# A two-layer hybrid decoder trunk on eight cores: hand-ordered engine queues with stage barriers replaced by one graph of operations under a static list scheduler

## The chip, the cores and the metric

The program runs on the 8 cores of one Trainium2 chip, one batch element per core; the cores do not talk to each other. The time is the device time of the slowest core, in microseconds (us). Fast runs of one kernel mostly agree within about 0.4%. Some runs fall into a slower state, in which the cores of one die, or of both, show a lower clock of the tensor engine. Only fast runs are compared here unless the text says otherwise.

Engines are named as in the profile: PE does matmuls, PEld loads their weights, DVE is VectorE, ACT is ScalarE, POOL is GpSimd, SP issues DMAs. PEclk is the clock granted to PE, as a share of full speed. The trace's clock records begin with a kernel's first dense work (at 183.6 us in the kernel before); ahead of that a view prints 1.00, which is not a measurement.

## The reference, cut to what matters

Each core has x of 4096 positions by 1024 features in fp32. Matmuls are in bf16, sums in fp32. The kernels work in 8 tiles of 512 positions and in four stages, called here M0 (mixer of layer 0), F0 (its MLP), M1 (mixer of layer 1) and F1 (second MLP and final norm).

```python
def reference(x, c, ada_w, ada_b, ...):
    for layer in range(DEPTH):                                   # DEPTH = 2
        sh1, sc1, g1, sh2, sc2, g2 = ada_modulation(c, ada_w[layer], ada_b[layer])   # silu(c) @ (1024 x 6144)
        h = rmsnorm(x, norm_mix_g[layer]) * (1.0 + sc1) + sh1
        if layer % 2 == 0:
            p = jnp.einsum('bsd,de->bse', h, w_in0[j])           # 3584 columns
            a_b, a_c, a_h, b_q, b_f, b_i, b_g = jnp.split(p, IN0_SPLITS, axis=-1)
            y_a = short_conv_mixer(a_b, a_c, a_h, conv_w[j], conv_b[j])
            y_b = hgrn2_mixer(b_q, b_f, b_i, b_g, lower_bounds[layer], hg_gain[j])
            y = jnp.einsum('bse,ed->bsd', jnp.concatenate([y_a, y_b], axis=-1), w_out0[j])
        else:
            z = jax.nn.gelu(jnp.einsum('bsd,de->bse', h, w_in1[j]) + b_in1[j])
            y = spatial_gating_mixer(z, gm_ln_g[j], gm_ln_b[j], gm_ws[j], gm_bs[j])
            y = jnp.einsum('bse,ed->bsd', y, w_out1[j])
        x = x + g1 * y
        h = rmsnorm(x, norm_ffn_g[layer]) * (1.0 + sc2) + sh2
        hid = jnp.square(jax.nn.relu(jnp.einsum('bsd,df->bsf', h, w_ff1[layer])))    # 4096 columns
        x = x + g2 * jnp.einsum('bsf,fd->bsd', hid, w_ff2[layer])
    return rmsnorm(x, final_g)
```

HGRN2 is a gated linear recurrence in chunks of 64 positions. Within a chunk it needs the running sum `cum` of the log forget gates, and the products of queries and keys with `exp(cum)`, `exp(-cum)` and `exp(last - cum)`.

## The kernel before

Operations are put on five queues, one per engine, **in the order in which the Python program makes them**. Each waits for the semaphores of what it reads and overwrites. Overlap is what the author wrote by hand with generators, and every stage ends with a barrier that only weight loads may cross.

```python
class Prog:
    def op(self, qn, fn, reads=(), writes=(), dsem=None):
        q = self.q[qn]
        for b in reads:
            if b.w is not None:
                self._wait(qn, b.w)
        for b in writes:
            for t in b.r.values():
                self._wait(qn, t)
            if b.w is not None:
                self._wait(qn, b.w)
        # ... (cut: append to the queue, count the semaphore up, set b.w and b.r)
```

The RMSNorm (L366 squares, a matmul with a constant matrix that sums over features, L376 scaling on VectorE, L379 shift on ScalarE):

```python
        def norm_and_modulate(xT, xTb, sqt, sqb, tmp, tmpb, hT, hb, invB, b_inv, ...):
            for c in range(8):
                P.op("act", lambda e, ...: e.activation(out=sqt[:, c % 2, :], in_=src_ap, func=AF.Square),
                     reads=[src_b], writes=[sqb[c % 2]])
                P.op("pe", lambda e, c=c: mm(e, ps[:, nbank, :], onesD[:], sqt[:, c % 2, :], c == 0, c == 7), ...)
            rsqrt_eps(invB[:], b_inv, ps[:, nbank, :], b_norm_bank)
            for c in range(8):
                P.op("dve", lambda e, c=c: e.scalar_tensor_tensor(
                    out=tmp[:, c % ntmp, :], in0=xT[:, c, :], scalar=scol(l, which, c), in1=invB[:],
                    op0=ALU.mult, op1=ALU.mult), ...)
                P.op("act", lambda e, c=c: e.activation(out=hT[:, c, :], in_=tmp[:, c % ntmp, :], func=AF.Identity, ...)
```

The MLP computes the next tile's norm between two halves of its own matmuls, so that part of it is hidden (L865 relu, L867 square of it):

```python
                    ff2(0, xT, xTb)
                    for _ in ff1(1):
                        pass
                    if ti + 1 < ntiles:
                        norm_and_modulate(xT2[:, 1 - cur], xTb2[1 - cur], ...)     # next tile
                    ff2(1, xT, xTb)
```

The adaLN modulation is a prologue of 24 pieces of 2 MB of fp32 weights that ends before anything else starts (a barrier follows it). The HGRN2 gates make every decay by its own subtraction, clipping and exponential; per head and tile that is one scan and eleven full-size VectorE passes, and seven ScalarE passes:

```python
                        P.op("dve", ... S_ft[:, 0] = cum3 - cum3[:, :, 63:64] ...)      # to the chunk's end
                        P.op("act", ... S_ft[:, 0] = Exp(-S_ft[:, 0]) ...)
                        P.op("dve", ... S_kd = S_ft[:, 2] * S_ft[:, 0] ...)
                        P.op("dve", ... S_ft[:, 1] = cum4 - S_cref2 ...)                # to the middle of the chunk
                        P.op("act", ... S_ft[:, 1] = Exp(S_ft[:, 1]) ...)
                        # ... (cut: two more of this kind, then q times two of the factors)
```

(The argument lists are shortened to formulas in this last block.) x comes in position-major and is transposed on PE in fp32 (L494), and transposed back at the end (L897).

The softmax here doesn't subtract the row's maximum and nothing guards it: scores larger than these inputs give would overflow.

## Time and profile before

| | |
|---|---|
| time | 4312.05 us, median of 3 runs (4309.94 to 4314.02) |
| profiled span, slowest core | 4319.8 us |
| PE busy, mean granted clock | 73%, 0.85 |

From the page of the kernel before: busy time and share of the span per engine; the span in 40 slices, with the busy tenths of PE and the tenths of the granted clock; and last the chain of work that ended last, by engine.

```profile
PE 3138.2 (73%) x15143; PEld 1426.2 (33%) x15143; DVE 1577.8 (37%) x3025; ACT 1302.1 (30%) x2085; POOL 60.4 (1%) x75
PE   1166465475564649999999975757664999999997
PEclk9887677686676769999999997878877999999998
PE 62%; ACT 11%; DVE 10%; DMA 9%; issue 7%; DVEq 0%; ACTq 0%; POOL 0%; SPq 0%; POOLq 0%
```

The tensor engine has the most work, but it is idle a quarter of the time, and 15 of the 40 slices show a clock digit of 7 or 6. The chain says that 62% of the span is PE's own work; the rest of the chain is other engines' work, DMA and issue.

Busy time of each engine in eight stretches of the kernel before: prologue, M0, change, F0, change, M1, change, F1. The columns are the stretch and its length, busy us and instructions of PE, PEld, DVE, ACT and POOL, then granted clock, DMA share and GB/s.

```profile
0.00:165.00 165.00, 23.48 (x738) 21.84 (x738) 2.36 (x13) 2.99 (x4) 21.33 (x28) 1.00 1.12 157
165.00:1542.00 1377.00, 788.33 (x3968) 370.14 (x3968) 653.19 (x1273) 507.36 (x800) 15.40 (x18) 0.73 0.16 36
1542.00:1570.00 28.00, 0.00 (x0) 0.00 (x0) 0.00 (x0) 0.00 (x0) 3.19 (x5) 0.56 0.88 198
1570.00:2571.00 1001.00, 935.97 (x4160) 410.44 (x4160) 249.73 (x448) 243.71 (x400) 7.49 (x9) 0.95 0.17 44
2571.00:2600.00 29.00, 1.88 (x6) 0.92 (x6) 4.36 (x11) 1.58 (x3) 0.00 (x0) 0.53 0.79 235
2600.00:3244.00 644.00, 422.76 (x1856) 182.22 (x1855) 317.51 (x640) 288.96 (x415) 4.97 (x6) 0.79 0.17 51
3244.00:3290.00 46.00, 4.42 (x8) 0.83 (x8) 1.66 (x3) 7.35 (x12) 4.26 (x6) 0.51 1.01 223
3290.00:4320.00 1030.00, 961.34 (x4408) 439.79 (x4408) 348.98 (x638) 250.11 (x452) 3.71 (x5) 0.95 0.13 37
```

The mixers are the loose stages: in M0 PE is busy 788 of 1377 us at clock 0.73. The MLPs are nearly dense. The changes cost 28, 29 and 46 us. Per tile the stages take about 170 (M0), 122.9 (F0), 78.6 (M1) and 125.8 us (F1).

The longest of PE's waits in the kernel before (engine, tile, line, and what ended the wait: us in total, times, longest).

```profile
PE ps L220 <- DVE sb_arena L1104: 160.0, 47, 7.8
PE ps L220 <- ACT sb_arena L366: 156.1, 121, 38.0
PE ps L220 <- DMA sb_arena<-ada_w: 136.6, 24, 7.3
```

L1104 is the spatial gating of M1, L366 are the squares of the norm, and `ada_w` is the prologue. They are serial chains; the change supposes that PE could do other work in the meantime, if the queue order let it.

### The profile page before, as it was taken

The numbers are of one execution on the slowest core, as the hardware profiler recorded it, in microseconds if no ns is written. First come the engines' busy times: TensorE is split into PE (matmuls) and PEld (weight loads), VectorE is DVE, ScalarE is ACT, GpSimd is POOL, SyncE is SP. The second block draws the span as 40 slices with busy tenths as digits, with TensorE's granted clock in tenths as the row PEclk, the third lists the DMA queues.
The fourth block names the chain that finished last, engine by engine and source line by source line (L and its number), as shares of the span: only waits on it lengthen the run. The fifth ranks groups of instructions, "written<-read, shape, count | busy, mean of one in ns | idle before, by whom it ended". The sixth has DMA issues, their size and how long they took to land.

```text
span 4319.8 us, 45196 instructions; the slowest of 8 cores (4287.9 to 4319.8 us)
## 1 busy us (share of the span) xinstructions
PE 3138.2 (73%) x15143; PEld 1426.2 (33%) x15143; DVE 1577.8 (37%) x3025; ACT 1302.1 (30%) x2085; POOL 60.4 (1%) x75
## 2 busy tenths in 40 slices
PE   1166465475564649999999975757664999999997
PEld 1132232232222214444444432323222444444443
DVE  0154444444444522222222214454551333333333
ACT  0143333433433422222222204444531222222221
POOL 1100000000000000000000000000000000000000
PEclk9887677686676769999999997878877999999998
DMA  9920010010001470011111230211139001111100
GB/s 157 160 50 20 20 40 20 20 39 20 20 20 39 69 145 21 20 40 39 40 40 40 48 74 29 75 39 60 58 61 178 15 25 40 40 40 40 40 16 25
DMA packets 126001, 213.73 MB, mean 49 GB/s; under 512 B 2640, under 2 KB 59728, under 8 KB 125776
## 3 DMA queue, kind: packets, MB, share of 16 engines
q0 software_dynamic: 65648, 74.45, 11.9%
q1 hardware_dynamic: 60128, 136.39, 9.0%
q8 instruction: 128, 2.10, 0.2%
q14 instruction: 97, 0.79, 0.1%
HBM read 218.17 MB, written 67.11 MB: 66 GB/s over the span
## 4 chain that ended last, share of the span: by engine, by line
PE 62%; ACT 11%; DVE 10%; DMA 9%; issue 7%; DVEq 0%; ACTq 0%; POOL 0%; SPq 0%; POOLq 0%
PE ps L220 61%; DMA sb_arena<-ada_w 3%; DMA xs<-sb_arena 2%; ACT sb_arena L366 2%; DVE sb_arena L1104 2%; DVE sb_arena L733 2%; DVE sb_arena L376 2%; ACT sb_arena L379 1%; DMA sb_arena<-x 1%; DMA sb_arena<-xs 1%; DMA sb_arena<-w_in 1%; ACT sb_arena L214 1%; ACT sb_arena L216 1%; ACT sb_arena L737 1%; PE ps L897 1%
## 5 line engine op out<-in xcount | busy, mean ns | idle before, releaser
L220 PE MATMUL ps<-sb_arena 128*128 128x512 bf16 (+4 forms) x14209 | 2899.1, 365 | 809.2 <-DVE sb_arena L1104 160.0
L220 PEld LDWEIGHTS ps<-sb_arena 128*128 128x128 bf16 x14209 | 1307.8, 102 | 2387.4 <-issue 1072.5
L865 ACT ACTIVATE sb_arena<-ps 128x512 bf16<-128x512 f32 x512 | 303.1, 596 | 1262.6 <-PE ps L220 1231.5
L867 DVE TENSOR_TENSOR sb_arena<-sb_arena 128x512 bf16<-128x512 bf16 x512 | 215.7, 425 | 615.5 <-ACT sb_arena L865 615.5
L883 DVE SCALAR_TENSOR_TENSOR sb_arena<-ps,sb_modc,sb_arena 128x512 f32<-128x512 f32 x256 | 190.8, 750 | 590.2 <-PE ps L220 590.1
L376 DVE SCALAR_TENSOR_TENSOR sb_arena<-sb_arena,sb_s1c 128x512 f32<-128x512 f32 x256 | 186.9, 750 | 384.0 <-ACT sb_arena L216 256.8
L366 ACT ACTIVATE sb_arena<-sb_arena 128x512 bf16<-128x512 f32 x256 | 147.2, 620 | 345.1 <-PE ps L494 171.6
L220 PE MATMUL ps<-sb_arena,sb_onesD 128*128 128x512 bf16 x256 | 131.2, 540 | 160.7 <-ACT sb_arena L366 156.1
L379 ACT ACTIVATE sb_arena<-sb_arena,sb_modc 128x512 bf16<-128x512 f32 x256 | 181.2, 722 | 162.7 <-DVE sb_arena L376 161.3
L220 PEld LDWEIGHTS ps<-sb_arena,sb_onesD 128*128 128x128 bf16 x256 | 26.4, 104 | 262.1 <-issue 262.1
L737 ACT ACTIVATE sb_arena<-sb_arena 128x512 bf16<-128x512 f32 x64 | 40.3, 629 | 216.7 <-DVE sb_arena L733 216.7
L1104 DVE SCALAR_TENSOR_TENSOR sb_arena<-ps,sb_vcol,sb_arena 128x128 f32<-128x128 f32 x256 | 89.5, 350 | 20.8 <-DVE sb_arena L1104 0.9
L733 DVE SCALAR_TENSOR_TENSOR sb_arena<-sb_arena,ps 128x128 f32<-128x128 f32 x256 | 88.2, 345 | 20.4 <-PE ps L220 0.3
L494 PE MATMUL ps<-sb_consts,sb_arena 128*128 128x128 f32 x256 | 60.7, 414 | 41.0 <-DMA sb_arena<-x 40.0
L1069 DVE TENSOR_TENSOR sb_arena<-ps,sb_arena 128x512 f32<-128x512 f32 x64 | 43.4, 689 | 119.5 <-PE ps L220 119.5
L220 PE MATMUL ps<-sb_arena,sb_ones 128*128 128x512 bf16 x32 | 18.8, 586 | 86.6 <-ACT sb_arena L768 86.6
L545 ACT ACT_TABLE_LOAD x16 | 20.5, 1283 | 199.5 <-DMA xs<-sb_arena 190.4
L804 DVE SCALAR_TENSOR_TENSOR sb_arena<-ps,sb_modc,sb_arena 128x512 f32<-128x512 f32 x64 | 48.1, 751 | 89.1 <-PE ps L220 89.1
L1139 DVE SCALAR_TENSOR_TENSOR sb_arena<-ps,sb_modc,sb_arena 128x512 f32<-128x512 f32 x64 | 47.4, 749 | 68.0 <-PE ps L220 68.0
L214 ACT ACTIVATE sb_arena<-sb_arena,sb_epsc 128x1 f32<-128x1 f32 x64 | 18.8, 295 | 164.5 <-DVE sb_arena L906 121.5
L494 PEld LDWEIGHTS ps<-sb_consts,sb_arena 128*128 128x128 f32 x256 | 49.4, 217 | 47.8 <-issue 47.0
L528 DVE SCALAR_TENSOR_TENSOR sb_arena<-sb_arena,sb_vcol 128x512 f32<-128x512 f32 x64 | 48.1, 751 | 35.7 <-ACT sb_arena L523 32.4
(102 smaller groups left out, 1421.7 us busy)
## 6 DMA issues: line engine op xcount, KB each, us to landing
xs<-sb_arena SPq DMA_DIRECT2D x24, 2048.0 KB, 8.0
sb_arena<-xs SPq DMA_DIRECT2D x24, 2048.0 KB, 9.2
sb_arena<-w_ff POOLq DMA_DIRECT2D x32, 1024.0 KB, 22.6
sb_arena<-ada_w POOLq DMA_DIRECT2D x24, 1024.0 KB, 18.1
sb_arena<-x SPq DMA_DIRECT2D x8, 2048.0 KB, 8.8
out<-sb_arena SPq DMA_DIRECT2D x32, 512.0 KB, 2.7
sb_arena<-w_in POOLq DMA_DIRECT2D x11, 1024.0 KB, 21.1
sb_arena<-w_out POOLq DMA_DIRECT2D x4, 1024.0 KB, 17.5
```

The lines of the kernel that those rows point to most:

```text
L214: P.op("act", lambda e: e.activation(out=out_ap, in_=in_ap, func=AF.Ln, bias=epsc[0:out_ap.shape[0], :], scale=1.0), reads=[in_buf, b_smal ...
L220: return e.matmul(out, lhsT, rhs, start=start, stop=stop)
L366: P.op("act", lambda e, c=c, src_ap=src_ap: e.activation(out=sqt[:, c % 2, :], in_=src_ap, func=AF.Square), reads=[src_b], writes=[sqb[c % ...
L376: P.op("dve", lambda e, c=c: e.scalar_tensor_tensor(out=tmp[:, c % ntmp, :], in0=xT[:, c, :], scalar=scol(l, which, c), in1=invB[:], op0=A ...
L379: P.op("act", lambda e, c=c: e.activation(out=hT[:, c, :], in_=tmp[:, c % ntmp, :], func=AF.Identity, bias=mod(l, shift_grp, c), scale=1.0 ...
L494: ins = e.transpose(out=ps[:, bk, g * 128:(g + 1) * 128], in_=xin[:, g, c * 128:(c + 1) * 128], identity=ident)
L733: P.op("dve", lambda e, j=j, ci=ci: e.scalar_tensor_tensor(out=Sst[:, j * 128:(j + 1) * 128], in0=Sst[:, j * 128:(j + 1) * 128], scalar=el ...
L737: P.op("act", lambda e, nxt=nxt: e.activation(out=Sb[:, nxt, :], in_=Sst[:], func=AF.Copy), reads=[b_S], writes=[Sbb[nxt]])
L865: P.op("act", lambda e, fc=fc, bk=bk: e.activation(out=rt[:, fc % 2, :], in_=ps[:, bk, :], func=AF.Relu), reads=[bank[bk]], writes=[rtb[fc ...
L867: P.op("dve", lambda e, fc=fc, fcl=fcl: e.tensor_tensor(out=hid[:, fcl, :], in0=rt[:, fc % 2, :], in1=rt[:, fc % 2, :], op=ALU.mult), read ...
L883: P.op("dve", lambda e, c=c, bk=bk: e.scalar_tensor_tensor(out=xT[:, c, :], in0=ps[:, bk, :], scalar=mod(l, 5, c), in1=xT[:, c, :], op0=AL ...
L1104: P.op("dve", lambda e, cc=cc, ec=ec, hh=hh, bk=bk: e.scalar_tensor_tensor(out=t1[:, hh, cc * 128:(cc + 1) * 128], in0=ps[:, bk, cc * 128: ...
```

## The change

The intent: one graph for the whole program. Operations are added with what they read and write, with an assumed duration and with a priority key, which is roughly the time at which the author wants it. A list scheduler then simulates the engines and gives each free engine the ready operation of lowest key. There are no barriers. PSUM banks are allotted by the scheduler, up to a limit per class.

```diff
-class Prog:
-    def op(self, qn, fn, reads=(), writes=(), dsem=None):      # program order
+class Graph:
+    def add(self, eng, parts, reads=(), writes=(), key=0.0, occ=0.2, lat=None, table=None, dsem=None, nbytes=0):
+        ...
+        for b in reads:
+            self._read(op, b, 0.0, op.pdeps[0])
+        for b in writes:
+            ...
+            for d in b.r:                                       # who read it before, in order of construction
+                self._dep(op, d, False, 0.0, op.pdeps[0])
+            if b.w is not None:
+                self._dep(op, b.w, True, 0.0, op.pdeps[0])
+    def schedule(self, limits, log=None):
+        ...
+        while left:
+            now = heapq.heappop(events)[0]
+            for e in engs:
+                while free[e] <= now + 1e-9 and avail[e]:
+                    ...                                         # lowest key among the ready ones
+                    if pick.nbytes:
+                        s0 = max(dma_free, st + pick.occ + 1.0)
+                        dma_free = s0 + pick.nbytes / 280e3
+                        pick.fin = dma_free + 1.2
 ... (cut)
-                load_xs(xT2[:, 0], xTb2[0], 0, d_ld[0])
-                norm_and_modulate(xT2[:, 0], xTb2[0], sqt, sqb, tmp, tmpb, hT, hb, invB, b_inv, bank[4], 4, l, 1)
+            for ti in range(ntiles):
+                b = base + TF * ti
+                hT, hb = hT0, hT0b
+                stage_a(ph, ti, hT, hb, b - 60, b - 45)         # load x, square, sum, scale
+                if l == 0 and ti < 8:
+                    for c in range(6):
+                        ada_piece(1, ti * 6 + c, b + 10 + 15 * c)
+                for fc in range(32):
+                    ...                                         # first projection, relu, square
+                for c in range(8):
+                    ...                                         # second projection, residual
+                if final:
+                    k = b + TF
+                    Bn = bank("norm")
+                    norm_stats(lambda c: (xf[:, c, :], xfb[c]), Bn, inv2, b_inv2, k)
+                    ...                                         # scale and store
 ... (cut: HGRN2)
-                        # eleven full VectorE passes and seven ScalarE passes per head
+                    act(... t_ = Tanh(0.5 * p) ...)
+                    act(... L_ = Ln(t_ * lbc + lbc') ...)
+                    dve(... tensor_tensor_scan ...)
+                    act(... E_ = Exp(L_) ...)
+                    dve(... L_ = max(L_, -85) ...)
+                    act(... L_ = Exp(-L_ + bias) ...)
+                    dve(... K_ = (t_ - 1) * L_ ...)
+                    pool(... KB_ = K_ * block factor ...)
+                    dve(... kd_ = K_ * block factor ...)
+                    dve(... Q_ = -q * E_ ...)
+                    pool(... Qe = Q_ * block factor ...)
```

The block factors are `exp(cum)` at positions 31 and 63 of a chunk, and their product: one exponential of `cum` and one of `-cum` serve all decays. Further: x arrives and leaves feature-major, so the fp32 transposes go; the state's decay goes to GpSimd; adaLN weights come in 96 pieces of 512 KB of fp32 through a ring of four, only 16 of them ahead of the first tile, the others spread over M0 and F0.

Two helpers matter for the argument. `norm_stats` is used by every norm and has two buffers for squares, `sqt[:, c % 2]`, shared by all of them:

```python
        def norm_stats(get, Bn, dst, b_dst, key):
            for c in range(8):
                ap, b = get(c)
                act(lambda e, c=c, ap=ap: e.activation(out=sqt[:, c % 2, :], in_=ap, func=AF.Square),
                    [b], [sqb[c % 2]], key, c_act(512))                                              # L625
                pe([(lambda e, c=c: e.matmul(bk(Bn), onesD, sqt[:, c % 2, :], start=c == 0, stop=c == 7),
                     [sqb[c % 2], b_onesD], c_mm(512))], [Bn], key)                                  # L627
            # ... (cut: Ln and Exp give the inverse root)
        def stage_a(ph, ti, hT, hb, key_sq, key_h):
            # ... (cut: load xT, L638)
            norm_stats(lambda c: (xT[:, c, :], xTb[c]), Bn, inv, b_inv, key_sq)
            # ... (cut: per feature block, L645 scaling on VectorE, L649 shift on ScalarE into hT)
```

Lines of the kernel after: L550 weight load, L591 and L598 adaLN load and matmul, L671 projection group, L774 and L797 gates on VectorE, L792, L807 and L900 products on GpSimd, L1010 second MLP projection, L1149 product of M1 on GpSimd, L1156 M1's output projection.

## The prediction

> **What bounds the kernel now.** Times per stage, read from when the activation stores are issued (timeline of the sync engine): adaLN prologue 0–165 us, layer-0 mixer 165–1542 (one 512-position tile per 170 us), first MLP to 2571 (122.9 per tile), second mixer to 3244 (78.6 per tile), second MLP to 4320 (125.8 per tile). Barriers between stages idle PE 30–50 us. In steady MLP work the first-projection groups follow each other every 1.727 us (timeline of VectorE), that is 216 ns per 512-column matmul at granted clock 1.0. So 12,033 large matmuls need only 2,598 us. The rest is waiting or running slow: busy time by stretch shows the mixer of layer 0 with PE busy 57% and clock 0.73, the second mixer 66% and 0.79, the MLPs 93% and 0.95. PE's waits name serial chains (HGRN2 gates, state, norm; RMSNorm squares 156 us; gating 160 us) and adaLN weights (137 us). The Trainium skill, "TensorE: Matmul & The Clock Gate", Part 1, says an idle window of about 3.4 us halves the clock; this trace agrees: the clock takes only the values 0.5 and 1.0, and every halving lies in such a hole (10 us at each MLP tile, 78 us of each mixer tile).
>
> **What the change does.** One graph, ordered by a static scheduler whose assumed durations match this trace (ScalarE 0.60–0.72, VectorE 0.69–0.75, squared ReLU 0.42 us). Next tile's norm, projections, recurrence and previous tile's output projection interleave; no barriers; only 16 of 96 adaLN pieces precede the first tile. Input and output arrive feature-major, so 512 fp32 transposes (97 us of PE) go. HGRN2 loses about six VectorE and one or two ScalarE passes per head, part goes to GpSimd: 34 us estimated per tile of about 80, off the critical path unless it is twice as slow. ScalarE table loads rise from 98 to 146 (1.283 us each): about 60 us, hidden.
>
> **Cost afterwards.** PE work: 12,384 matmuls of 512 columns at 216 ns = 2,675 us, plus about 2,300 small ones at 30–65 ns = 100 us: floor 2,775. Add start 45 (8 MB of adaLN weights at the 340 GB/s that the prologue shows, then one norm), 20 for input weights arriving one 2 MB piece per 6 us, 25 at three stage changes, 50 of holes in mixer 0, 25 in mixer 1, 20 for the last tile's norm and store, 40 for orders that miss real durations: **2980 us**. By stage, per tile: mixer 0 170→86, MLPs 123–126→112–113, mixer 1 78.6→49. Nearly all of it is on the critical path.
>
> Range 2860 to 3200 (8 in 10). Faster by over 2%: 0.97; within 2%: 0.01; slower: 0.02.
>
> **What shows it right.** PE busy at least 93% outside the first 50 us, clock 1.0 nearly throughout, instead of 0.85; chain of waits mostly PE matmuls; no tenth below 8 at the stage changes; MLP tiles 112–113 us.
>
> **What would make it wrong.** (1) The same page says that dense matmuls on three or more cores of a die bring the clock to 13/16; the MLP stages before, dense for 116 us, show no such value, so I expect none, but milliseconds of dense work could: then about 3,400. (2) GpSimd slower than estimated, or slowing VectorE, so that the gates or state hold PE in mixer 0 (over 95 us per tile). (3) MLP weights late at stage changes: holes above 20 us each.

## The result, and the profile after

The kernel after took **3282.23 us** (median of 4 runs, 3280.88 to 3287.95); the kernel before in the same rounds took 4313.03 us (4 runs, 4309.94 to 4326.69). The ratio is 0.761 (95% interval 0.759 to 0.762). A ratio here is always the mean time of one kernel's fast runs over that of the other's of the same rounds, so it is not quite the ratio of the quoted medians. Faster by far, as predicted, but 302 us slower than the predicted 2980 us and 82 us above the upper end of the range.

From the page of the kernel after: the same four lines as for the kernel before.

```profile
PE 2900.0 (88%) x14693; PEld 1306.0 (40%) x14693; DVE 1161.0 (35%) x1898; ACT 1248.9 (38%) x1910; POOL 426.8 (13%) x563
PE   0699999986899999999995889878898898988988
PEclk9999999987999999999997999989898998988989
PE 76%; DMA 8%; ACT 6%; DVE 5%; issue 4%; another core or an unknown queue 1%; POOL 0%; DVEq 0%; ACTq 0%; SPq 0%; POOLq 0%
```

PE is busy 88% (73% before), and the chain is now 76% PE. The picture by slices shows where it is not: the first slice is empty, slices 22 to 27 (the change to M1, and M1) are mostly at 8 and below, and the last thirteen (F1) alternate between 8 and 9. Before, F1 was nines.

Busy time in five stretches of the kernel after: start, M0, F0, M1, F1. The columns are those of the stretches before.

```profile
0.00:109.80 109.80, 11.19 (x139) 5.82 (x140) 11.71 (x44) 16.23 (x26) 15.46 (x34) 1.00 0.99 177
109.80:778.50 668.70, 613.89 (x4043) 294.97 (x4041) 426.29 (x589) 462.83 (x683) 300.53 (x413) 0.96 0.45 105
778.50:1717.00 938.50, 909.31 (x4438) 414.39 (x4436) 203.28 (x417) 226.80 (x373) 19.02 (x36) 0.98 0.31 78
1717.00:2180.00 463.00, 375.84 (x1794) 168.28 (x1793) 263.39 (x389) 256.85 (x359) 80.51 (x69) 0.89 0.46 123
2180.00:3281.40 1101.40, 989.78 (x4288) 422.51 (x4287) 256.30 (x461) 286.22 (x471) 11.27 (x12) 0.92 0.19 55
```

The stages against before and against the prediction, in us. A stage is counted from the end of the one ahead, so the changes are inside; for the kernel before each is the change and the stage together. The prediction's column is its per-tile figure times 8, with its terms for start, input weights and last tile.

| stretch | before | predicted | after | after minus predicted |
|---|---|---|---|---|
| start to first dense group | 165 | 45 + 20 = 65 | 109.8 | +45 |
| M0 | 1377 | 688 (86 a tile) | 668.7 (steady tiles 79) | -19 |
| F0 | 1029 | 900 (112.5 a tile) | 938.5 | +38 |
| M1 | 673 | 392 (49 a tile) | 463 | +71 |
| F1 | 1076 | 900 + 20 | 1101.4 | +181 |
| stage changes | inside | 25 | inside | -25 |

(The predicted column adds up to 2990, not 2980, since the per-tile figures are rounded; the last column to 291.) The largest miss is F1, which did not get faster at all: 1101 us against 1076. It has the same projections as F0. One steady tile of F1 and one of F0 in the kernel after, in the same columns:

```profile
2482.00:2614.00 132.00, 122.09 (x528) 51.97 (x528) 30.57 (x56) 36.57 (x61) 0.00 (x0) 0.93 0.15 48
1100.00:1212.00 112.00, 112.00 (x528) 50.77 (x527) 25.34 (x49) 30.50 (x50) 0.53 (x1) 1.00 0.19 59
```

Both hold 528 matmuls (512 of the projections and 8 of the next norm in both; the other 8 are the final norm's sums in F1, and one-column adaLN matmuls in F0), and VectorE and ScalarE are far from full in both. F0 is dense for 112 us at clock 1.00; F1 takes 132 us.

The longest of PE's waits in the kernel after, in the first fence over the whole span, in the second within F1 (2350 to 3270 us) alone:

```profile
PE ps L598 <- DMA sb_arena<-ada_w: 114.3, 13, 31.7
PE ps L627 <- ACT sb_arena L625: 112.7, 70, 25.3
PE ps L671 <- ACT sb_arena L649: 40.6, 35, 3.6
```

```profile
PE ps L671 <- ACT sb_arena L649: 34.7, 29, 3.6
PE ps L627 <- ACT sb_arena L625: 28.9, 48, 2.7
```

In F1 PE waits for the squares (L625) and for the shifted norm output (L649), over and over. The order in which it happens is in the timeline of PE at one tile boundary of F1 (start us, length, engine and line, tile, count, and in brackets the idle time before and what ended it):

```profile
2473.73 1.46 PE L1010 MATMUL ps<-sb_arena 128*128 128x512 bf16 x6
2475.02 0.59 PE L627 MATMUL ps<-sb_arena 128*128 128x512 bf16 x2
...
2479.21 2.56 PE L627 MATMUL ps<-sb_arena 128*128 128x512 bf16 x4 [0.69 <-ACT sb_arena L625]
2483.00 1.11 PE L627 MATMUL ps<-sb_arena 128*128 128x512 bf16 x2 [1.24 <-ACT sb_arena L625]
...
2490.45 1.25 PE L671 MATMUL ps<-sb_arena 128*128 128x512 bf16 x2 [3.32 <-ACT sb_arena L649]
```

The last second-projection matmuls of one tile end at 2475. Then come sixteen L627 sums. The first eight are the *final* norm of that tile, the other eight the norm of the *next* tile; the four at 2479.21 are two of each. The next tile's first projection starts at 2490.45, 15 us after the last matmul of its tile ahead, and the granted clock is 0.5 for 17 to 20 us at each such boundary. The Trainium skill's page on TensorE, cited in the prediction, has such a halving follow an idle window of about 3.4 us; this trace differs. Its clock records turn to 0.5 at 2479.8 us, where PE had been busy 1.9 of the last 3.4 us and no gap in the ten us before was longer than 0.71 us; the idle 3.32 us come only afterwards. (At 2498 us matmuls still start 427 ns apart, and after 2500.3 us, where the records are back at 1.0, 216 ns apart, so the records fit the work.) In the kernel before, too, most halvings at MLP tile boundaries follow gaps of at most 1.47 us. The priorities asked for something else: `stage_a` of the next tile has the key b - 60, 60 us ahead of its tile. F0, where no final norm exists, does just that. In F1 the next tile's squares stand behind the final norm's at the two shared buffers, and the final norm cannot end before the tile's last projection does, whatever its key.

The start of the kernel after, again as timelines: first GpSimd's DMA issues, then PE.

```profile
1.55 2.26 POOL L591 DMA_DIRECT2D sb_arena<-ada_w  x4 [0.84 <-POOLq L401]
3.78 2.14 POOL L550 DMA_DIRECT2D sb_arena<-w_in  x4
11.15 0.53 POOL L591 DMA_DIRECT2D sb_arena<-ada_w  x1 [5.23 <-PE ps L598]
11.67 1.60 POOL L550 DMA_DIRECT2D sb_arena<-w_in  x3
13.22 1.09 POOL L550 DMA_DIRECT2D sb_arena<-w_out  x2
```

```profile
54.52 0.35 PE L598 MATMUL ps<-sb_arena 128*128 128x1 bf16 x8 [26.81 <-DMA sb_arena<-ada_w]
86.58 0.35 PE L598 MATMUL ps<-sb_arena 128*128 128x1 bf16 x8 [31.70 <-DMA sb_arena<-ada_w]
...
109.84 2.72 PE L671 MATMUL ps<-sb_arena 128*128 128x512 bf16 x6
```

The ring gives room for four adaLN pieces. While the fifth waits for the first one's matmul, the scheduler issues input weights (`w_in`, `w_out`): their keys are later, but they are ready and nothing else is. The fifth and sixth group of adaLN matmuls then wait 27 and 32 us: adaLN pieces land in a median of 4.9 us over the whole run, but the fifth, asked for behind four weight pieces, took 43.2 us, and the later ones stand behind nine, at a DMA share of 0.99. The Trainium skill, "DMA: Bandwidth & Descriptors", section "Issuing engines are not separate DMA queues", says that all DMAs run on the same 16 engines and interleave whoever issues them. This start does not test that, since GpSimd issues both kinds; experiment 4 below agrees with it, where loads of x issued by SP took up to 29.4 us beside weights issued by GpSimd.

Two more holes, both in PE's timeline of the kernel after: in F0's first tile, and between F0 and M1.

```profile
829.39 0.35 PE L598 MATMUL ps<-sb_arena 128*128 128x1 bf16 x8 [29.19 <-DMA sb_arena<-ada_w]
...
1742.29 1.11 PE L627 MATMUL ps<-sb_arena 128*128 128x512 bf16 x2 [25.25 <-ACT sb_arena L625]
```

The first one is an adaLN piece of layer 1, hoisted into the middle of the MLP weight loads. In the second one PE waits for a square, which waits for its input, which waits for a place: M1's constants were put in memory that only F0's last operations free.

### The profile page after: what moved, and what is told of

Its sections match the earlier page's. It is cut to its first block, busy times and chain, and to the rows that moved or that the text cites. A ratio compares the mean times of both kernels' runs of the same rounds, so it can differ in the third digit from the quotient of the medians.

```text
span 3281.4 us, 41979 instructions; the slowest of 8 cores (3261.0 to 3281.4 us)
## 1 busy us (share of the span) xinstructions
PE 2900.0 (88%) x14693; PEld 1306.0 (40%) x14693; DVE 1161.0 (35%) x1898; ACT 1248.9 (38%) x1910; POOL 426.8 (13%) x563
## 4 chain that ended last, share of the span: by engine, by line
PE 76%; DMA 8%; ACT 6%; DVE 5%; issue 4%; another core or an unknown queue 1%; POOL 0%; DVEq 0%; ACTq 0%; SPq 0%; POOLq 0%
PE ps L671 36%; PE ps L1010 27%; DMA sb_arena<-ada_w 4%; PE ps L1104 3%; PE ps L1156 3%; PE ps L960 2%; DVE sb_arena L645 2%; DMA xs<-sb_arena 2%; PE ps L627 2%; ACT sb_arena L625 1%; DMA sb_arena<-xs 1%; ACT L392 1%; DMA sb_arena<-x 1%; PE ps L840 1%
## 5 line engine op out<-in xcount | busy, mean ns | idle before, releaser
L671 PE MATMUL ps<-sb_arena 128*128 128x512 bf16 x6144 | 1405.3, 386 | 56.1 <-ACT sb_arena L649 40.6
L671 PEld LDWEIGHTS ps<-sb_arena 128*128 128x128 bf16 x6144 | 599.2, 99 | 804.2 <-issue 119.9
L1010 PE MATMUL ps<-sb_arena 128*128 128x512 bf16 x4096 | 891.9, 379 | 0.0
L1010 PEld LDWEIGHTS ps<-sb_arena 128*128 128x128 bf16 x4096 | 399.3, 98 | 481.5
L625 ACT ACTIVATE sb_arena<-sb_arena 128x512 bf16<-128x512 f32 x320 | 190.5, 621 | 691.3 <-PE ps L627 480.2
L662 DVE SCALAR_TENSOR_TENSOR sb_arena<-ps,sb_arena 128x512 f32<-128x512 f32 x192 | 142.8, 746 | 489.3 <-PE ps L1010 343.5
L645 DVE SCALAR_TENSOR_TENSOR sb_arena<-sb_arena 128x512 f32<-128x512 f32 x256 | 223.6, 906 | 79.2 <-ACT sb_arena L631 61.7
L627 PE MATMUL ps<-sb_arena 128*128 128x512 bf16 x320 | 135.3, 437 | 116.9 <-ACT sb_arena L625 112.7
L649 ACT ACTIVATE sb_arena<-sb_arena 128x512 bf16<-128x512 f32 x256 | 179.5, 720 | 144.4 <-DVE sb_arena L602 74.3
L392 ACT ACT_TABLE_LOAD x146 | 187.3, 1283 | 47.1 <-PE ps L671 21.0
L1020 DVE SCALAR_TENSOR_TENSOR sb_arena<-ps,sb_arena 128x512 f32<-128x512 f32 x64 | 48.1, 751 | 390.6 <-PE ps L1010 390.6
L591 POOL DMA_DIRECT2D sb_arena<-ada_w x96 | 53.2, 555 | 926.4 <-PE ps L627 548.5
L1156 PE MATMUL ps<-sb_arena 128*128 128x512 bf16 x512 | 125.1, 388 | 23.9 <-POOL sb_arena L1149 23.9
L1104 PE MATMUL ps<-sb_arena 128*128 128x512 bf16 x512 | 135.2, 413 | 10.0 <-ACT sb_arena L649 9.6
L598 PE MATMUL ps<-sb_arena 128*128 128x1 bf16 x768 | 32.7, 165 | 115.6 <-DMA sb_arena<-ada_w 114.3
L1149 POOL TENSOR_TENSOR sb_arena<-sb_arena 128x512 bf16<-128x512 f32 x64 | 82.6, 1303 | 371.0 <-DVE sb_arena L1144 370.8
L960 PE MATMUL ps<-sb_arena 128*128 128x512 bf16 x512 | 121.7, 394 | 2.0 <-DVE sb_arena L946 2.0
L627 PEld LDWEIGHTS ps<-sb_arena 128*128 128x128 bf16 x320 | 31.5, 99 | 184.7 <-issue 168.1
L900 POOL TENSOR_TENSOR sb_arena<-sb_arena 128x512 f32<-128x512 f32 x64 | 75.3, 1177 | 93.0 <-DVE sb_arena L904 91.5
L1104 PEld LDWEIGHTS ps<-sb_arena 128*128 128x128 bf16 x512 | 52.8, 104 | 85.8 <-issue 36.1
```

What stands on the lines that cost most here:

```text
L392: eng.preload_act_table_set(op.table)
L625: act(lambda e, c=c, ap=ap: e.activation(out=sqt[:, c % 2, :], in_=ap, func=AF.Square), [b], [sqb[c % 2]], key, c_act(512))
L627: pe([(lambda e, c=c: e.matmul(bk(Bn), onesD, sqt[:, c % 2, :], start=c == 0, stop=c == 7), [sqb[c % 2], b_onesD], c_mm(512))], [Bn], key)
L645: dve(lambda e, c=c: e.scalar_tensor_tensor(out=tmp[:, c % 2, :], in0=xT[:, c, :], scalar=s1c[:, q, c:c + 1], in1=inv, op0=ALU.mult, op1=A ...
L649: act(lambda e, c=c: e.activation(out=hT[:, c, :], in_=tmp[:, c % 2, :], func=AF.Identity, bias=mod(l, g, c), scale=1.0), [tmpb[c % 2], mo ...
L671: parts = [(lambda e, kc=kc: e.matmul(bk(B), w[:, kc, col0:col0 + 128], hT[:, kc, :], start=kc == 0, stop=kc == 7), [wb, hb[kc]], c_mm(512 ...
```

## The experiments

The theory was that four separate things, none of them an engine's speed, make up the miss: **(C)** the construction order of the two norms in F1, **(A)** the input weights ahead of the adaLN pieces at the start, **(B)** the adaLN pieces of layer 1 in F0's first tile, **(D)** the place of M1's constants. Rivals: VectorE or ScalarE are too slow beside GpSimd, or the scheduler's assumed DMA times are too short in general. All kernels gave results within the reference's tolerance. In all, 15 kernels ran. The times below are medians of a kernel's fast runs; experiments 1 to 5, 7, 8 and 15 start from the kernel after (4 includes the edit of 3), 6 combines 1, 2, 4 and 5, and 9 to 14 build on 6. Lengths of tiles are read from the first gate function (M0), relu (F0, F1) or gelu (M1) of one tile to that of the next.

### 1. Next tile's norm built before the final norm (C)

```diff
-                stage_a(ph, ti, hT, hb, b - 60, b - 45)
+                if ti == 0 or not final:
+                    stage_a(ph, ti, hT, hb, b - 60, b - 45)
 ...
+                if final and ti + 1 < ntiles:
+                    stage_a(ph, ti + 1, hT, hb, b + TF - 60, b + TF - 45)
                 if final:
                     k = b + TF
                     Bn = bank("norm")
```

No operation and no key changes. Only the order of construction does, and by it, who waits for whom at the two shared buffers for squares.

> The changed kernel takes 132 us per tile in the last MLP and 112.5 us in the first one, which does the same matmuls. Theory: the norm of the next tile is held back behind the final norm of this tile by a dependency that is only bookkeeping: both write the same two square buffers, and buffers are granted in the order in which the graph was built, whatever the priorities say. This kernel only builds the next tile's norm ahead of the final norm. Theory expects 113 to 115 us per tile, no half-clock stretch at the tile boundary, and 3282 - 7 x 18 = about 3150 us. Rival: the work of the final norm (8 squares, 8 matmuls, a serial tail on ScalarE) can't be hidden; then at least 125 us per tile and over 3230 us.

Measured: 3189.91 us, ratio to before 0.7385 (0.7365 to 0.7405), 92 us less than the kernel after. This repair alone brings the time inside the predicted range. One steady F1 tile of this kernel, columns as for the stretches:

```profile
2370.00:2487.00 117.00, 114.78 (x529) 51.55 (x528) 30.25 (x57) 35.63 (x60) 0.00 (x0) 1.00 0.19 54
```

The tile goes from 132 to 117 us (up to 118.8), and the clock stays at 1.00. Six steady tiles at about 14 us give some 83 us. The first tile becomes 38 us shorter, but starts 27 us later, since a new hole of 23.6 us appeared at the change from M1 to F1. The theory is right: the order at the shared buffers, fixed at construction, held F1; not the next norm's key, and no engine's speed. Its size came out smaller than expected: the final norm's eight sums (some 1.7 us at 216 ns) and about 2 us of small gaps stay in every tile.

### 2. Input weights held behind the adaLN pieces (A)

```diff
-                win[i] = load_weight(i, "win%d" % i, "k", win0_d[i], -25.0 + n)
+                win[i] = load_weight(i, "win%d" % i, "k", win0_d[i], -25.0 + n,
+                                     ada_ops[9] if n == 0 else ada_ops[15])
 ... (cut: w_out likewise; load_weight makes the given matmul group a dependency of the load)
```

> TensorE starts dense work at 110 us instead of the 65 that I had allowed. Theory: nine weight pieces of 2 MB were issued ahead of twelve of the sixteen adaLN pieces of the first norm, which wait in the DMA queue behind 18 MB (two waits of 27 and 32 us). Here the weight pieces wait for adaLN work (the first for piece 10, the others for piece 16). Theory expects the first dense matmul at 50 to 60 us and 3225 to 3240 us in all. Rival: the first tile needs all of these bytes anyway, so the order only moves the wait into the first tile, and the time stays over 3265 us.

Measured: 3246.80 us (0.7523; 0.7504 to 0.7541), 35 us less. The first gate function on ScalarE starts at 69.0 instead of 114.8 us, 46 us earlier. A quarter of that is given back later. The theory holds in kind; dense work starts at 64.5 us, not at 50 to 60, and the time is 7 us above what it expected.

### 3. Later keys for the adaLN pieces of layer 1 (B, first form)

```diff
-                    for c in range(6):
-                        ada_piece(1, ti * 6 + c, b + 10 + 15 * c)
+                    for c in range(8 if 1 <= ti <= 6 else 0):
+                        ada_piece(1, (ti - 1) * 8 + c, b + 5 + 13 * c)
```

> The first tile of the first MLP takes about 37 us longer than the others, and PE stands 29 us in front of an adaLN piece of layer 1 whose load queues behind the MLP weights. Here no adaLN piece lies in that tile (8 in each of tiles 1 to 6). Theory: the in-order queue of PE was blocked by work that nobody needed yet; expects the hole to go, 3245 to 3260 us. Rival: the MLP weights themselves arrive late and PE would wait for them at the same time; then the hole stays under another name and the time stays over 3270 us.

Measured: 3283.68 us (0.7612), no change. The longest of PE's waits from 760 to 930 us in this kernel:

```profile
PE ps L598 <- DMA sb_arena<-ada_w: 29.3, 1, 29.3
```

The hole is still there to the microsecond. This was a flawed test of (B), and still of use: the pieces' keys said tile 1 or later, yet they were issued ahead of tile 0's work, since the DMA-issuing queue had nothing else ready. This scheduler leaves no engine idle while anything is ready, so a key cannot hold an operation back.

### 4. The same pieces held by a dependency (B, second form)

```diff
+                        ada_piece(1, (ti - 1) * 8 + c, b + 5 + 13 * c, hold)
 ...
+                    if ti == 0:
+                        hold = G.ops[-1]          # after the last first-projection group of tile 0
```

> The run before this one changed only the priority of the adaLN pieces of layer 1, and the scheduler, which never leaves a free queue idle, still placed four of them in the first MLP tile: the hole of 29 us stood there unchanged, again named after an adaLN piece. So that run did not test the theory. Here the loads of those pieces depend on the last first-projection group of that tile. Theory (PE blocked by a piece nobody needs yet, queued behind the MLP weights, which have landed by then in part): first MLP tile about 120 us instead of 149, 3250 to 3260 us. Rival (the MLP weights themselves are late): a hole of over 20 us stays under the name of the weights, over 3270 us.

Measured: 3256.62 us (0.7524; 0.748 to 0.7567), 26 us less. F0 starts 24 us earlier, but its first tile goes only from 149 to 141.8 us, not to 120. The theory is partly right: the hole named `ada_w` is gone, and behind it stood another. The longest of PE's waits from 740 to 900 us in this kernel:

```profile
PE ps L674 <- DVE sb_arena L665: 13.3, 2, 12.6
```

L665 is the residual add of M0's last tile. It waits for pieces of x of 256 KB. The loads of that line land in 3.2 us in the median of this run, but the four issued from 774 to 797 us took 12.6 to 29.4 us, beside the 32 MB (fp32) of MLP weights.

### 5. M1's constants in memory that is free early (D)

```diff
-            reg = Region([(6 * SLOT, 8 * SLOT), (A_HID, A_HID + 32768), (A_RT, A_RT + 2048),
-                          (A_XF + 8192, A_XF + 16384), (15 * SLOT, 16 * SLOT), (con.spans[0][0], NBYTES)])
+            reg = Region([(6 * SLOT, 8 * SLOT), (A_HID, A_HID + 32768),
+                          (15 * SLOT, 16 * SLOT), (con.spans[0][0], NBYTES)])
+            ereg = Region([(A_XF + 8192, A_XF + 16384)])
+            RB, b_RB = tile(ereg, "RB", [128, 8, 128], F32)
+            wmT, b_wm = tile(ereg, "wmT", [128, 4, 128], BF16)
 ... (cut: the bias in two halves; tile 0 uses the other hT buffer)
```

> At the change from the first MLP to the second mixer PE stands 25 us and then runs half-clocked. Theory: the constants of the mixer are prepared in the buffer of the next input tile but written into memory of the MLP's hidden layer, so the input tile can be loaded only after the last MLP matmul. Here these results lie in memory that is free earlier and the first tile uses the free activation buffer; expects the hole of 25 us and most of the ramp after it to go: 3240 to 3255 us. Rival: the input tile comes late because 14 MB of weight loads are issued just ahead of it; then the hole stays and the time is over 3270 us.

Measured: 3262.18 us (0.7562; 0.7549 to 0.7575), 20 us less. The first gelu of M1 starts at 1738 instead of 1760 us, and the hole of 25 us is gone: PE's longest wait at this change is 3.4 us. The theory holds for the hole; the time is 7 us above what it expected.

### 6. All four together

> The four repairs together: weights behind the first adaLN pieces, adaLN of layer 1 held until the first MLP tile's first projection is done, the second mixer's constants in memory that is free early, the next tile's norm built ahead of the final norm. If the holes are independent the gains add: 92 + 34 + 29 + 20 us, so about 3105 us. Rival: the loads at the stage changes compete for the same DMA time, so a hole that is closed opens again behind it; then over 3150 us.

Measured: 3095.23 us (0.715; 0.7109 to 0.7191). The four gains alone (92, 35, 26 and 20) would give 3109, so they add, with 14 us to spare. The stages were: M0 79 us a tile, F0 139 for the first tile and then 113.8, M1 54.2 to 56.1 (first 69.9), F1 117 to 118.8 (first 153). The four causes together are 187 of the 302 us missed. M1's first tile became longer than in the kernel after (69.9 against 50.7 us); experiment 14 takes that up.

### 7. The same graph in program order

The scheduler may only give each engine its next operation in order of construction; the graph, the operations and the bank limits are unchanged.

```diff
+        prog = {e: [op.id for op in self.ops if op.eng == e][::-1] for e in engs}
+        for op in self.ops:
+            op.key = 0.0
 ...
+                    if avail[e][0][1] != prog[e][-1]:
+                        break
```

> The same operations, buffers and bank rules, but every engine takes its operations in the order in which the graph was built: no list scheduling. Theory: the reordering is the larger part of the gain over the kernel before, because each tile's serial chains (gates, state, norm) are hidden only under another tile's matmuls; expects 3750 to 4050 us, mixer 0 at over 120 us per tile and MLP tiles over 123. Rival: the gain is mostly removed work (fp32 transposes, HGRN2 passes, the barriers, most of the adaLN prologue), which stays removed here; expects under 3550 us.

Measured: slower than the kernel before. The two fast runs took 4808.24 and 4811.02 us (ratio to before 1.111; 1.102 to 1.120). Both theories' figures were missed: without reordering all of the gain is lost and more. A likely reason, not tested, is that this graph's construction order has none of the hand-made interleaving of the kernel before; so the run shows that this graph needs its scheduler, not what a scheduler gains over hand-made order. From the profiled run, a slow one, the tiles took about 192 us (M0), 133 (F0), 96 (M1) and 162 us (F1).

### 8. Barriers between the stages

Every first operation of a stage (weight loads excepted) depends on the last ones of the stage ahead; the scheduler is as in the change.

> The changed kernel with a barrier between the four stages (weight loads excepted): no operation of a stage starts before the stage ahead of it has ended. Theory: a barrier costs what the kernel before showed at its stage changes, 28 to 46 us each with the ramp of the first norm, of which part is already lost here to late loads: 3340 to 3400 us. Rival: the stage changes are bound by the weight loads and not by the missing overlap; then under 3310 us.

Measured: runs of 3364, 3374 and 3395 us (0.7801; 0.7728 to 0.7875). The last, the profiled one, was disturbed: die 1 shows clocks of 0.918 to 0.925 against 0.932 on die 0. The other two are 82 and 92 us over the kernel after, some 30 us for each of three barriers, as theory had it.

### 9 to 12. What is left after the four: DMA, or VectorE

The first MLP tiles and M1 were still above plan. Two theories: weights that come too many at a time hold up small loads (the rival: the weights are needed just as urgently), and M1's tile is held by VectorE, which GpSimd slows.

"Two in flight" adds to experiment 6 that a weight piece is issued only after the one two ahead of it has landed. "All DMA" adds instead that the scheduler counts on slower DMA:

```diff
-                        dma_free = s0 + pick.nbytes / 280e3
-                        pick.fin = dma_free + 1.2
+                        dma_free = s0 + pick.nbytes / 200e3
+                        pick.fin = dma_free + 3.5
```

> The four repairs left 3097 us. What remains at the stage changes (first MLP tile 139 us against 114, first tile of the second mixer 70 against 54, first tile of the last MLP 153 against 118) is put down to small loads (the residual pieces of 256 KB and the input tile) that wait in the DMA queue behind many weight pieces of 2 MB. Here, on top of the four repairs, a weight piece is asked for only when the piece two before it has landed. Theory: the small loads wait for two pieces (13 us) at most; the three first tiles lose 10 to 20 us each: 3040 to 3070 us. Rival: those tiles need the weights themselves at the full rate of the DMA, and two in flight are slower or the same: over 3090 us.

> The four repairs, and the scheduler assumes slower DMA (200 instead of 280 KB per us, 3.5 instead of 1.2 us of latency): no operation changes, only the order. In the second mixer PE stands 5.8 us per tile in front of a norm matmul whose square waits for the next input tile, whose load takes 5.9 us at the median where the scheduler assumes about 4. Theory: the order was made from too short a load, so with longer ones the norm is placed later and the hole goes: second mixer 50 us per tile instead of 54, in all 3050 to 3075 us. Rival: the load starts late, for the buffer comes free late, and it is not its assumed duration that counts: 54 us per tile stay, over 3085 us.

Measured: two in flight took 3103.21 us against the 3095.23 of experiment 6, no gain. From the first relu of F0's first tile to that of the second it is 108.6 instead of 139 us, as the theory wants, but only because the first tile's second projection has moved behind that relu (353 matmuls stand in this stretch, 840 in the next, of 185 us). The last of its weights are asked for at 802.5 us and it runs from 825.7. The two stretches together take 294 us against 253 in experiment 6: the rival is right. With slower assumed DMA, the fast runs took 3118 and 3119 us, and M1 became worse (59 to 60 us a tile). Slower assumed DMA throughout does not help.

Experiment 11 moves M1's product from GpSimd to VectorE (`pool(...)` at L1149 becomes `dve(...)`, with a dependency that keeps the order).

> The four repairs, and the gating multiply of the second mixer runs on VectorE instead of GpSimd. Beside GpSimd's multiply the scale operation of the next tile's norm on VectorE takes 1.15 us instead of 0.75, so the input buffer comes free late and the load behind the 5.8 us hole starts late. Theory: the hole is from this slowing; that operation returns to 0.75 us in this stage and the tile takes 49 to 51 us: 3055 to 3075 us. Rival: the single input buffer makes the hole (free, load 6 us, square), whatever VectorE's speed: 53 us or more per tile, over 3085 us.

Measured: 3090.86 us, which is within the noise of experiment 6. The scaling of the norm on VectorE, from 1700 to 2100 us, first in this kernel, then in that of experiment 6 (line, engine, operation, tile and shapes, count | busy us, mean ns | idle before and what ended it):

```profile
L653 DVE SCALAR_TENSOR_TENSOR sb_arena<-sb_arena 128x512 f32<-128x512 f32 x64 | 45.5, 746 | 12.2 <-ACT sb_arena L657 5.5 <-ACT sb_arena L639 4.4 <-ACT sb_arena L1140 1.5
```

```profile
L653 DVE SCALAR_TENSOR_TENSOR sb_arena<-sb_arena 128x512 f32<-128x512 f32 x64 | 63.8, 1032 | 13.9 <-ACT sb_arena L639 9.7 <-ACT sb_arena L657 3.7 <-ACT sb_arena L1139 0.4
```

The same instruction takes 746 ns without GpSimd's products beside it and 1032 ns with them. The Trainium skill, "SBUF — State Buffer", section "Who interferes with whom", says that a VectorE instruction with two SBUF inputs contends with a GpSimd instruction that reads SBUF; this pair of runs shows it, as 38% in the mean. And yet the tile only went from 54.3 to 53.4 us: the contention is real and lies off the critical path of this kernel, in which the norm's key is still late.

> The four repairs, two weight pieces in flight, the slower DMA assumed by the scheduler and the multiply on VectorE, together: if each of the three helps as its theory says, 2990 to 3040 us; if their rivals hold, 3090 us again.

Experiment 12, the edits of 9 to 11 together, took 3122.86 us: together they are slower than the four repairs alone.

### 13. M1's norm with an earlier key

In M1, unlike in experiment 3, the operation was ready and merely passed over: the keys of the next tile's norm were only 32 and 20 us ahead of their tile.

```diff
-                stage_a(2, ti, hT, hb, b - 32, b - 20)
+                stage_a(2, ti, hT, hb, b - 50, b - 44)
```

> On top of the four repairs and the multiply on VectorE, the norm of the next tile in the second mixer gets an earlier priority (50 and 44 us ahead of its tile instead of 32 and 20). Theory: its input tile lies loaded for 20 us before its squares run, so the hole of 5 us per tile, in which PE waits for the modulated activations, comes from a priority that is too late, not from the single buffer; expects 48 to 51 us per tile instead of 53.4 and 3050 to 3075 us in all. Rival: the single input buffer limits it; 53 us stay and the time stays over 3085 us.

Measured: 3052.72 us (0.7062; 0.7043 to 0.7081), 38 us less than experiment 11, on which it is built. The longest of PE's waits, for the squares, in M1 (1770 to 2040 us) of experiment 11, then (1770 to 2010 us) of this one:

```profile
PE ps L635 <- ACT sb_arena L633: 38.3, 7, 8.8
```

```profile
PE ps L635 <- ACT sb_arena L633: 6.4, 4, 3.8
```

The wait falls from 38.3 to 6.4 us, and the tile from 53.4 to 45 or 46 us (some 51). The late key was the cause; the rival, that a single buffer of x held it, falls. Whether the key alone would do, with the product back on GpSimd, was not run.

### 14. F1's first weights one at a time

The eight loads of F1's first projection each wait for the one ahead (added to experiment 13), so that they do not come all at once beside M1's small loads.

> The same, and the first-projection weights of the last MLP, which have 450 us to arrive, are loaded one at a time instead of seven at once at the start of the second mixer. Theory: the first tile of that mixer (69 us against 53) waits for its next input tile behind these seven pieces; expects that tile at 55 to 58 us and 10 to 15 us less than the run before in this call. Rival: no change within 5 us.

Measured: **3030.43 us** (0.7013; 0.6997 to 0.7029), 22 us less, where 10 to 15 had been expected. The first M1 tile went from 71 to 43.5 us. It beats both kernels: 0.70 of the time before, and 252 us, or 7.7%, less than the kernel after. Its five stretches, cut as for the kernel after, take 65, 647, 938, 410 and 970.8 us. The last two, M1 and F1, with columns as before:

```profile
1650.00:2060.00 410.00, 385.65 (x1920) 179.03 (x1919) 284.80 (x464) 236.07 (x350) 8.40 (x14) 0.97 0.58 147
2060.00:3030.80 970.80, 927.81 (x4222) 414.30 (x4220) 241.85 (x443) 271.41 (x455) 1.16 (x3) 0.98 0.18 58
```

What remains above plan is known by place but was not tested: F0's first tile (about 27 us), F1's first tile (158.8 us, about 40 over), and some 5 us in each F1 tile for the final norm.

### 15. Six VectorE passes put back into the gates

Each gate chain of the kernel after gets six needless full-size passes on VectorE, in line with the rest.

```diff
+                    for _ in range(6):
+                        dve(lambda e, L_=L_: e.tensor_tensor(out=L_, in0=L_, in1=L_, op=ALU.max), [b_L], [b_L], k,
+                            c_dve(512))
```

> The changed kernel without repairs, with six more VectorE passes of 0.69 us in the gate chain of every head (results unchanged): about what the block factors had taken out of HGRN2. Theory: with the scheduler's overlap PE, not VectorE, limits mixer 0, so the removed passes were worth little by themselves: 78 us per tile become at most 83, in all under 3330 us. Rival: the gate chain is what mixer 0 waits for, so 4 heads x 4.1 us = 16 us per tile come back: over 3390 us.

Measured: 3332.29 us (0.771; 0.7693 to 0.7728), 50 us over the kernel after, 2 us beyond what was expected as the most. M0's tiles went from 79 to about 83 us, the first from 57 to 72. So the lighter HGRN2 algebra is worth some 50 us of the 1031 us won, at least as far as VectorE's passes go and under this scheduler. The three ScalarE passes were not put back.

## Why the prediction was right or wrong

**Right: the direction, and the reason.** The kernel before was held by waiting and by the half clock that follows, not by work. The chain of waits went from 62% to 76% PE, the mean clock from 0.85 to 0.944. In program order (experiment 7) this graph loses all of it, and barriers alone (experiment 8) cost 82 to 92 us.

**Right: M0.** Predicted 86 us a tile, measured 79. GpSimd was busy 37.6 us a tile (300.5 us in the whole stage) against the 34 estimated; its two-input products take 1.17 to 1.31 us. The Trainium skill, "GPSIMD Engine Reference", section "4.1 Engine selection", says about twice VectorE's time for two inputs; this case agrees, with 1303 ns for M1's product on GpSimd and 683 ns for it on VectorE in experiment 11. VectorE is slowed beside it, as risk (2) said (experiment 11). None of that held PE over 95 us a tile. The prediction's count of passes was low, too: "about six VectorE and one or two ScalarE passes per head" are seven and three in the code.

**Right: no clock of 13/16.** Risk (1), that clock under eight dense cores, did not come in this kernel: up to 887 us without a break at 1.0. Of all runs classed fast that were profiled, one shows it, on one die (experiment 8).

**Wrong: "MLPs 123–126→112–113", for both.** This is the step that failed most. F0 kept it in its steady tiles (112.4 us, dense), F1 did not (132 us), and F1 with its end was 181 us over. The prediction took it that the next tile's norm interleaves in both, and its sum has the final norm only once, in "20 for the last tile's norm and store". It did not see that the final norm was built into the graph ahead of the next tile's norm and shares its two buffers of squares; the scheduler obeys that order as a data dependency. Building the two the other way round took 92 us off (experiment 1). Of the rest, some 44 us are the 5.5 us by which F1's repaired tile still exceeds F0's; what then remains was not taken apart.

**Wrong in size: "start 45" and "20 for input weights".** Measured 109.8 instead of 65. The prediction added the two as if adaLN pieces came first; in fact the input weights overtook them (experiment 2: 46 us earlier at the first gate).

**Wrong in size: "25 at three stage changes".** The holes of 29 us (F0) and 25 us (M1) alone are 54. Risk (3) had named it, "holes above 20 us each", but put it down to MLP weights. They were small loads behind bulk weights, and constants in memory that came free late (experiments 4 and 5: 26 and 20 us).

**Wrong in size: M1, "78.6→49".** Measured about 54.3 in steady tiles. A late key for the next norm made the difference (experiment 13: 45 to 46 us, with the product on VectorE).

**The general term "40 for orders that miss real durations" was the wrong kind of reserve.** What the experiments repaired lay in dependencies, in their absence and in one key; a slower DMA in the scheduler's model made it worse (3118 against 3095 us). That wrong durations cost nothing is not shown by this.

**The tests in its own words.** "PE busy at least 93% outside the first 50 us" was not met: it is 2894.7 of 3231.4 us, or 90% (91% outside the first 109.8 us). "No tenth below 8 at the stage changes" was not met either: slice 10 (M0 to F0) shows 6, slice 22 (F0 to M1) 5 and slice 27 (M1 to F1) 7. In experiment 14 PE is busy 2827.1 of 2980.8 us outside the first 50, or 95%, and that kernel's time lies within the predicted range. The prediction's floor of work was thus about right; it priced a kernel without these defects.

**Open.** How the 1031 us divide between overlap and removed work was not measured: PE's own busy time fell by 238 us, and experiment 15 prices VectorE's passes only. What the removed transposes and the three ScalarE passes are worth by themselves was not measured, nor was what remains in the first tiles of F0 and F1.

## What to carry to other kernels

Under a static list scheduler, look at what is *not* in the priorities: a shared scratch buffer gets its order when the graph is built and no priority can undo it, while a prefetch without a dependency is issued as soon as its queue is free, whatever its priority says. So build operations in the order you want for shared buffers, hold back bulk loads by a real dependency on what must come first, and then compare each stage's steady tile with that of a stage of equal work: 132 us against 112 us was visible in one line. A slower engine and contention between two engines were both real here, and moving the work between them gained nothing measurable (experiment 11); what waits last decides.

## What the Trainium skill lacked or had wrong

- "TensorE: Matmul & The Clock Gate", Part 1, says (measured there under the default power profile) that a third core of a die with dense matmuls brings the whole die to 13/16 within 5 to 20 us. All eight cores run dense at granted clock 1.0 for up to 887 us at a stretch in the kernel after, and none of the profiled runs but two shows the value 0.8125. One of the two is the slow run of experiment 7 (461 to 875 us on the cores of die 0, none on die 1), the other that of experiment 8 (129 to 270 us on the cores of die 1, none on die 0).
- The same Part 1 ties the halved clock to an idle window of about 3.4 us, and no page says how much work within a window keeps the clock up. In the kernel after the clock was halved seven times in F1 with no gap of PE above 0.71 us in the ten us before, and PE busy 1.9 to 2.1 of the last 3.4 us.
- "ScalarE: Activation LUTs", section "What ACT_TABLE_LOAD costs", gives about 1283 ns for a table load and 1380 ns more for a drain. The runs agree with the first (1283 ns, 146 loads, 187.3 us in the kernel after), but show no such drain: at 129.24 us a load of 1.28 us starts, at 130.54 the next activation, at 131.21 the next load.
- "SBUF — State Buffer" states the contention between VectorE and GpSimd, but gives no mean loss for a mix of work: here 746 against 1032 ns for a scalar_tensor_tensor of 128x512 fp32 in M1.
- "DMA: Bandwidth & Descriptors" says that all DMAs interleave on 16 engines, but gives no figure for small loads beside bulk ones: loads of 256 KB that land in 3.2 us in the median took up to 29.4 us beside weights (experiment 4).
- No page has anything on static scheduling: that a buffer's order of construction binds (14 us a tile in F1), and that a work-conserving scheduler hoists loads (a hole of 29.2 us in the kernel after is 29.3 us under later keys in experiment 3).
